# State update of the sample group: one matmul for each sample, on halves laid out by way of DRAM

## The chip, the cores and the metric

The kernel runs on one core of a Trainium2 chip. The metric is the device time of one execution in microseconds, the median of several runs. Engines are named as in the profile: PE is TensorE, DVE is VectorE, ACT is ScalarE, POOL is GpSimd, SP is SyncE, which here only issues DMAs.

## The reference

One layer of a hybrid decoder on 256 prompt tokens and 8 samples of 8 tokens each (64 sample tokens). An input projection of 2048 to about 13,000 columns feeds a Mamba-2 mixer (32 heads of 64, state 128, in 4 groups of 8 heads) and a gated short convolution; an output projection joins them. All is float32.

```python
h = rmsnorm(x, norm_w)
proj = jnp.einsum('bld,de->ble', h, w_in)
z_s, xbc, dt_raw, z_c, b_c, c_c, v_c = jnp.split(proj, SPLIT_POINTS, axis=-1)
xbc, buf_ssd_new = causal_dwconv(xbc, buf_ssd, conv_ssd_w)
xs, bm, cm = jnp.split(jax.nn.silu(xbc + conv_ssd_b), (D_SSM, D_SSM + SSD_GN), axis=-1)
y_s, h_new = ssd_scan(xs, dt, a, bm, cm, d_skip, h_ssm)
# inside ssd_scan:
states = jnp.einsum('bclgn,bclgh,bclghp->bcghpn', bc, decay_end, xdt)
h_next = h * chunk_decay + states
```

The last two lines are the state update that this case is about. For each sample b and each group g the new state is the old one times a decay, plus the sum over that sample's 8 tokens of the outer product of B (128 state columns) and the weighted x (512 columns, 8 heads of 64).

## The kernel before, in words

**Projections.** Tokens stand in the free dimension (256 + 64 = 320 columns). A product has one weight tile of 128 output columns and 16 steps of 128 along the contraction; each step is three matmuls (L175 to L177), since weights and activations are each split into a rounded part and a remainder (`wh`, `wl`; `xh`, `xl`) and three of the four cross products are taken. The weights come by SP's DMAs in halves of a tile (`wr`, three buffers, L150). ScalarE casts a quarter to `wh` (L159), VectorE subtracts to get `wl` (L160); six quarters of each can be held. So every quarter of every weight tile passes over SP, ScalarE and VectorE before TensorE can use it.

**Order of the work.** `schedule()` sets the order of the weight tiles: for each of the groups 0 to 3 the tiles B, C, x (four), z (four), and between them tiles of the short convolution (`sc`, `sv`, `sz`, `sb`). What a group's scan has to do stands in the generator `ssd_group`; `inproj` advances it by one `yield` at steps 5, 10 and 15 of each product (`tick`), so that the scan's small matmuls stand between those of the products. TensorE's order is that of the code. The other engines' order is set by the framework's scheduler, which moves instructions by its own costs; each engine and each DMA queue then works strictly in order.

**The scan of a group.** `padded` and `pad_samples` lay the 64 sample tokens out over 128 rows, each run of 16 tokens (two samples) twice: rows 0 to 15 of a quadrant of 32 and again rows 16 to 31. On these rows:
- `bt` is B transposed (tokens in rows). `Bst` holds, for each q in 0 and 1 (the even and the odd sample of a quadrant), B masked to that sample (`mq[q]`), as a rounded part and a negated remainder (ACT L595, DVE L596; 4 tiles of 128 x 128).
- `xw2` is the weighted x. `xst` has its rounded part in a quadrant's first 16 rows and the remainder in the last 16 (ACT L619 with the factor `sgn`, DVE L621 with `m1`).
- For each q, four matmuls `py` (L659) read the loaded old states `ht`, then for k = 0, 1 (rounded part and remainder of B) four matmuls `up` (L671), one in each quadrant of 32 rows, add up the update of four samples: two rounds of four. There is a block of this kind twice in a group, eight blocks in all.
- GpSimd multiplies `ht` by the decay (L675), VectorE adds `up` to `ht` (L682), GpSimd stores it (`out_hs`, L683).

**Around it.** SP also loads `ht` (`hload`, L554) and `R`, a row of cumulated decays broadcast to all rows (`rload`, L546). `rpart` turns R into decay factors: for the second chunk (c = 1) ScalarE takes an exponential into `CE` (L565) and GpSimd multiplies it by C (L566); then VectorE subtracts (L573, four heads to a tile), ScalarE takes the exponential (L576), VectorE multiplies by `CBm` (L577). `hf` is the prompt's final state, stored by `out_hp` (L653). In the same stretch stand the first short convolution's steps: `c` (L740), `pad` (L746, L748), `sa` (L753, L755), with GpSimd's copies L750 and L509.

Most of these 128 x 512 tiles come from one rotating pool of `NTR` = 12 tiles with the tag `tr` (`t5`, `small`).

Of the kernel before, what the change touches and what calls it, by code (L numbers as in the profile page):

```python
# [9 lines left out]
F32 = mybir.dt.float32  # L10
F32R = mybir.dt.float32r
AF = mybir.ActivationFunctionType
ALU = mybir.AluOpType
# [3 lines left out]
P = 128  # L17
# [3 lines left out]
NL = 8  # L21
TS = NB * NL
T = TP + TS
TQ = T // 4
KT = DM // P
H = 32
# [27 lines left out]

C_M1 = C_UP + TS
C_SG = C_M1 + 1
C_MQ = C_SG + 1
NC_ = C_MQ + 2

BEFORE = 2  # L60
BETWEEN = (1, 1, 1, 2)
# [3 lines left out]
NTR = 12  # L65
# [31 lines left out]
def hymba_step(ctx: ExitStack, tc: tile.TileContext, A, O):  # L97
    nc = tc.nc
    V, S, PE, GP, SP = nc.vector, nc.scalar, nc.tensor, nc.gpsimd, nc.sync

    def pool(name, bufs=1, **kw):
        return ctx.enter_context(tc.tile_pool(name=name, bufs=bufs, **kw))
# [6 lines left out]
    dr = pool("dram", space=DRAM)  # L109
# [4 lines left out]
    def bc(ap, shape):  # L114
        return ap.to_broadcast(shape)

    def win(t, at, *dims):

        v = t[:, at:at + 1]
        return bass.AP(v.tensor, v.offset, [v.ap[0], *[list(d) for d in dims]])  # L120
# [14 lines left out]
    def load(i):  # L135
        if i >= NTILE or i in raws:
            return
        got = []
        for hf in range(2):
            if i >= LATE and 2 * (i - LATE) + hf < 4 * NLATE - 3:  # L140
                r = keep[0].tile([P, KH, P], F32, name=f"wk{i}_{hf}")
            else:
                r = wp.tile([P, KH, P], F32, name=f"wr{i}_{hf}", tag="wr", bufs=3)
            if i < nin:
                src = A["w_in"][i, :, hf * KH:(hf + 1) * KH, :]
            else:
                d, part = divmod(i - nin, 2)
                k0 = part * KT + hf * KH
                src = A["w_out"][d, :, k0:k0 + KH, :]
            SP.dma_start(r, src)  # L150
            got.append(r)
        raws[i] = got
# [32 lines left out]
    xw = sp0.tile([P, KT, XW], F32, name="xw")  # L185
# [19 lines left out]
    load(NFIRST)  # L205
    con = cp.tile([P, NC_], F32, name="con")
    SP.dma_start(con, A["con"])
# [10 lines left out]
    UP = con[:, C_UP:C_UP + TS]  # L218
    m1 = con[:, C_M1:C_M1 + 1]
    sgn = con[:, C_SG:C_SG + 1]  # L220
    mq = [con[:, C_MQ + q:C_MQ + q + 1] for q in range(2)]
    cso = cp.tile([P, NXT, NB + 1, 3], F32, name="cso")
    sso = cp.tile([P, NSH, NB + 1, 2], F32, name="sso")
    ones = cp.tile([P, 1], F32, name="ones")
# [9 lines left out]
    for n in range(3):  # L234
        t = cp.tile([P, PW], F32, name=f"pad{n}")
# [35 lines left out]
    for k in range(KT):  # L271
        h = wp.tile([P, NFIRST * P], F32R, name=f"sh{k}", tag="wh", bufs=6)
# [112 lines left out]
    ssd = sst_.enter_context(tc.tile_pool(name="ssd", bufs=1, reuse_waits="tile"))  # L385
# [15 lines left out]
    acd = dr.tile([H, T], F32, name="acd")  # L401
    totd = dr.tile([H, NB + 1], F32, name="totd")

    seg = ssd.tile([H, T], F32, name="seg")
    GP.memset(seg, 1.0)
    GP.memset(win(seg, 0, (P, 2)), 0.0)
    GP.memset(win(seg, TP, (NL, NB)), 0.0)
    ges = ssd.tile([H, T], F32, name="ges")
    GP.memset(ges, 1.0)
    GP.memset(win(ges, P - 1, (P, 2)), 0.0)  # L410
    GP.memset(win(ges, TP + NL - 1, (NL, NB)), 0.0)
    CH = ((0, P, P), (P, P, P), (TP, TS, TS))

    def small(name, rows=H, cols=T):
        return ssd.tile([P, 512], F32, name=name, tag="tr", bufs=NTR)[:rows, :cols]

    def decays():

# [107 lines left out]
    def ssd_group(g, Bt, Ct, xs, zs):  # L526
# [3 lines left out]
        def t5(name, dt=F32):  # L530
            return ssd.tile([P, 512], dt, name=f"{name}_{g}", tag="tr", bufs=NTR)

        def tl(name):
            return ssd.tile([P, 512], F32, name=f"{name}_{g}", tag="tl", bufs=5)

        def rload(c, part):

            o, n, _ = CH[c]
            nh = 512 // n
            h0 = HPG * g + part * nh  # L540
            if (c, part) in PARTS[:2]:
                R = ssd.tile([P, 512], F32, name=f"R{c}_{part}_{g}", tag="rs", bufs=2)
            else:
                R = t5(f"R{c}_{part}")
            R = R.rearrange("p (h l) -> p h l", h=nh)
            SP.dma_start(R, bc(acd[h0:h0 + nh, o:o + n].rearrange("(u h) l -> u h l", u=1), [P, nh, n]))  # L546
            for h in range(nh):
                Rs[c, part * nh + h] = R, h

        hts = {}  # L550

        def hload(b):
            hts[b] = t5(f"ht{b}")
            SP.dma_start(hts[b], A["h"][g, :, b, :])  # L554
# [32 lines left out]
        p = sm(f"bt{g}")  # L587
# [2 lines left out]
        PE.transpose(p[:, 2 * P:3 * P], padded(Bt), ident)  # L590
        Btok = ssd.tile([P, 2 * P], F32, name=f"Btok{g}", tag="Btok")
        S.copy(Btok, p[:, :2 * P])
        Bst = ssd.tile([P, 2, 2, P], F32R, name=f"Bst{g}", tag="Bst")
        for q in range(2):
            S.activation(Bst[:, q, 0, :], p[:, 2 * P:3 * P], AF.Copy, scale=mq[q])  # L595
            V.scalar_tensor_tensor(out=Bst[:, q, 1, :], in0=p[:, 2 * P:3 * P], scalar=mq[q],  # L596
                                   in1=Bst[:, q, 0, :].bitcast(F32), op0=ALU.mult, op1=ALU.subtract)
        yield
        p = sm(f"cb{g}")
        CBm = ssd.tile([P, T], F32, name=f"CBm{g}", tag="CBm")  # L600
        for c, (o, n, _) in enumerate(CH):
            PE.matmul(p[:, o:o + n], Bt[:, o:o + n] if c < 2 else padded(Bt), Ct[:, o:o + n],
                      start=True, stop=True)
        V.tensor_tensor(out=CBm[:, :TP].rearrange("p (c l) -> p c l", c=2),
                        in0=p[:, :TP].rearrange("p (c l) -> p c l", c=2),
                        in1=bc(U.rearrange("p (o l) -> p o l", o=1), [P, 2, P]), op=ALU.mult)
# [4 lines left out]
        p = sm(f"xt2{g}")  # L611
# [3 lines left out]
        xw = t5("xw2")  # L615
        V.tensor_tensor(out=heads(xw, g), in0=heads(p, g), in1=perhead(w_tok[:, 2, hs]), op=ALU.mult)
        V.tensor_tensor(out=heads(xdt[2], g), in0=heads(p, g), in1=perhead(dt_tok[:, 2, hs]), op=ALU.mult)
        xh_ = t5("xh2", F32R)
        S.activation(xh_, xw, AF.Copy, scale=sgn)  # L619
        xst = ssd.tile([P, 512], F32R, name=f"xst{g}", tag="xst")  # L620
        V.scalar_tensor_tensor(out=xst, in0=xw, scalar=m1, in1=xh_.bitcast(F32), op0=ALU.mult, op1=ALU.add)  # L621
        yield
        rpart(0)
        yield
# [2 lines left out]
        for c in range(2):  # L627
            p = sm(f"xt{c}_{g}")
            for j in range(4):
# [3 lines left out]
                            in1=perhead(dt_tok[:, c, hs]), op=ALU.mult)  # L633
            xw = t5(f"xw{c}")
            V.tensor_tensor(out=heads(xw, g), in0=heads(p, g),
                            in1=perhead(w_tok[:, c, hs]), op=ALU.mult)
# [7 lines left out]
            p = sm(f"st{c}_{g}")  # L644
# [3 lines left out]
            else:  # L648
                hf = t5("hf")
                GP.tensor_tensor(out=heads(hf, g), in0=heads(h1, g),  # L650
                                 in1=decay(NB, g), op=ALU.mult)
# [5 lines left out]
        for q in range(2):  # L657
            for j in range(4):
                PE.matmul(py[32 * j:32 * j + 32, :], cz[:, 2 * j + q, :], hts[2 * j + q],  # L659
                          start=q == 0, stop=q == 1)  # L660
            if q == 0:
                for b in range(4):
                    hload(2 * b + 1)
            else:
                for part in PARTS[2:]:
                    rload(*part)
            ups = [sm(f"up{g}_{q}_{j}") for j in range(4)]
            for k in range(2):
                for j in range(4):
                    at = slice(32 * j, 32 * j + 32)  # L670
                    PE.matmul(ups[j], Bst[at, q, k, :], xst[at, :], start=k == 0, stop=k == 1)  # L671
            for j in range(4):
                b = 2 * j + q
                ht = hts[b]
                GP.tensor_tensor(out=heads(ht, g), in0=heads(ht, g),  # L675
                                 in1=decay(b, g), op=ALU.mult)
            yield
            yield
            for j in range(4):
                b = 2 * j + q  # L680
                ht = hts.pop(b)
                V.tensor_tensor(out=ht, in0=ht, in1=ups[j], op=ALU.add)  # L682
                GP.dma_start(O["hs"][g, :, b, :], ht)  # L683
                if j == 1:
                    yield
            yield
            yield
# [9 lines left out]
        for j in range(4):  # L697
            pd = sm(f"pd{g}_{j}")
            for c, (o, n, _) in enumerate(CH):
                for u in range(2):  # L700
                    h = 2 * j + u
                    PE.matmul(pd[u * HD:(u + 1) * HD, o:o + n], xdt[c][:, h * HD:(h + 1) * HD],  # L702
                              Rs[c, h][0][:, Rs[c, h][1], :], start=True, stop=c != 1)
                for u in range(2 * (c == 1)):
                    h = 2 * j + u
# [3 lines left out]
        for j, pd in enumerate(pds):  # L709
# [3 lines left out]
                                   in1=pd[:, :T], op0=ALU.mult, op1=ALU.add)  # L713
# [11 lines left out]
        v, a, b = (t5(f"{n}g")[:, :T] for n in "vab")  # L725
        yield from rms(acc, 4 * P, sm(f"rg{g}")[:, :T], [t5(f"acc{n}", F32R)[:, :T] for n in "hl"], v, a, b, b)
        yield
        for j in range(4):
            ct = 4 * g + j
            V.scalar_tensor_tensor(out=ysr[:, ct, :], in0=ys[j], scalar=vec[:, V_SN + ct:V_SN + ct + 1],  # L730
                                   in1=b, op0=ALU.mult, op1=ALU.mult)
# [53 lines left out]
    for i in [*range(2, NFIRST + NAHEAD), 0, 1, *range(NFIRST + NAHEAD, nin)]:  # L785
# [9 lines left out]
        if kind in "BC":  # L795
            t = ssd.tile([P, T + P], F32, name=f"{kind}{idx}", tag=kind, bufs=2)
# [4 lines left out]
        elif kind == "x":  # L801
            t = ssd.tile([P, T + P], F32, name=f"x{idx}", tag="xs", bufs=6)
# [58 lines left out]
    for d in range(KT):  # L861
        i = nin + 2 * d
        n = TP if i >= LATE else T
# [42 lines left out]
    t = tp.tile([P, T], F32, name="yt2", tag="yc")  # L906
    fnr, u, t = (a[late, :LW] for a in (fnr, u, t))
# [37 lines left out]
    for m, pt in enumerate(pts):  # L945
        at = slice(m * P, (m + 1) * P)
# [12 lines left out]
    for e, at in ((S, slice(0, half)), (SP, slice(half, 2 * half))):  # L959
        V.tensor_tensor(out=rs[:, at, :], in0=rs[:, at, :],  # L960
                        in1=bc(p3[:, :TS].rearrange("p (o t) -> p o t", o=1), [P, half, TS]), op=ALU.mult)
# [3 lines left out]
def constants():  # L965
    c = np.zeros((P, NC_), np.float32)
    i = np.arange(P)
    c[:, C_ID:C_ID + P] = np.eye(P)
    c[:, C_U:C_U + P] = i[:, None] <= i[None, :]
    t = np.arange(TS)  # L970

    tok, half = 16 * (i // 32) + i % 16, i // 16 % 2
    c[:, C_DI:C_DI + TS] = (half[:, None] == 0) & (tok[:, None] == t[None, :])
    c[:, C_UP:C_UP + TS] = (half[:, None] == 1) & (tok[:, None] // NL == t[None, :] // NL) & (tok[:, None] <= t[None, :])
    c[:, C_M1] = half
    c[:, C_SG] = 1 - 2 * half
    for q in range(2):
        c[:, C_MQ + q] = tok // NL % 2 == q
    return c


# [67 lines left out]
```

## Time and profile before

| | |
|---|---|
| median of 3 runs | 1027.83 us (1027.24 to 1028.45) |
| the profiled execution | 1028.2 us, its span 1026.4 us |
| TensorE clock granted | 0.998 |
| busy: PE, DVE, ACT, POOL | 1016.7, 671.5, 499.2, 199.8 us |
| DMA | 176.62 MB, 172 GB/s over the span |
| blocks of `py` and `up` | 8, from 143.5 to 491 us |

The profile is of one execution. Times of rows are microseconds from the start of the span; a duration of a single instruction is given in ns where it says so. In a timeline a row has start, length, engine, line, operation, the tile written and the tiles read, shapes, how many instructions were merged, and in brackets the engine's idle time before it and what ended it. A matmul's length is longer than the distance to the next one's start, since matmuls are pipelined. A wait is put down to what came last.

### The profile page before, as it was taken

To read this page: it belongs to the slowest core of one execution; us is meant where nothing else is said; L and a number is where in the kernel's file an instruction comes from. 1 tells how busy PE (TensorE), PEld (TensorE's weight loads), DVE (VectorE), ACT (ScalarE), POOL (GpSimd) and SP (SyncE) were. 2 spreads that over 40 slices of the span, in tenths; PEclk is the share of its full clock that TensorE was granted. 3 is DMA by queue.
4 is the path that set the end of the run, shared out by engine and by line. 5 is a ranking of instruction groups with operands and counts; after the bars stand their busy time and mean duration, and the time that the engine had idled before them with its cause. 6 is when DMAs were issued, how large, how long until landed. Compare 5 with 4: busy or idle time off the path is not lost.

```text
span 1026.4 us, 18690 instructions
## 1 busy us (share of the span) xinstructions
PE 1016.7 (99%) x7223; PEld 996.4 (97%) x7223; DVE 671.5 (65%) x1221; ACT 499.2 (49%) x901; POOL 199.8 (19%) x293
## 2 busy tenths in 40 slices
PE   9999999999999999999999999999999999999997
PEld 9999999999999989999999999999999999999996
DVE  7797767886978777886867555555556544444444
ACT  8476444663457444754445343443435544444450
POOL 0131034221522134224323100111111000000000
PEclk9999999999999999999999999999999999999999
DMA  9345474646473566458547444444445744544412
GB/s 370 126 135 180 145 264 167 185 143 227 167 224 124 195 217 212 137 167 257 186 150 244 158 146 154 153 144 154 155 145 156 259 150 145 154 154 145 149 37 103
DMA packets 63304, 176.62 MB, mean 172 GB/s; under 512 B 10496, under 2 KB 20352, under 8 KB 63088
## 3 DMA queue, kind: packets, MB, share of 16 engines
q1 hardware_dynamic: 59712, 164.98, 48.3%
q0 software_dynamic: 3072, 9.96, 2.7%
q8 instruction: 56, 0.92, 0.4%
q10 hardware_dynamic: 432, 0.49, 0.1%
q14 instruction: 32, 0.26, 0.1%
HBM read 162.83 MB, written 12.58 MB: 171 GB/s over the span
## 4 chain that ended last, share of the span: by engine, by line
PE 88%; DVE 5%; issue 3%; DMA 2%; POOL 1%; ACT 1%; DVEq 0%; SPq 0%; POOLq 0%; ACTq 0%
PE pj L176 20%; PE pj L175 20%; PE pj L177 20%; PE po L175 7%; PE po L177 7%; PE po L176 7%; PE pf L284 3%; DVE wl L160 1%; POOL ht L675 1%; DMA R<-acd 1%; PE pd L702 1%; DVE ht L682 1%; DVE R L573 1%; PE pt L918 1%; DVE R L577 1%
## 5 line engine op out<-in xcount | busy, mean ns | idle before, releaser
L160 DVE TENSOR_TENSOR wl<-wr,wh 128x512 fp32r<-128x512 f32 x518 | 364.8, 712 | 269.2 <-ACT wh L159 265.6
L159 ACT CAST wh<-wr 128x512 fp32r<-128x512 f32 x518 | 314.9, 618 | 387.5 <-PE pj L177 216.1
L175 PE MATMUL pj<-xh,wh 128*128 128x320 f32 x1600 | 499.6, 312 | 0.0
L176 PE MATMUL pj<-xh,wl 128*128 128x320 f32 x1600 | 493.8, 309 | 1.5 <-DVE wl L160 1.5
L177 PE MATMUL pj<-xl,wh 128*128 128x320 f32 x1600 | 493.2, 308 | 0.0
L175 PEld LDWEIGHTS pj<-xh,wh 128*128 128x128 f32 x1600 | 300.2, 188 | 5.6 <-issue 5.4
L176 PEld LDWEIGHTS pj<-xh,wl 128*128 128x128 f32 x1600 | 300.3, 188 | 4.6 <-DVE wl L160 2.7
L177 PEld LDWEIGHTS pj<-xl,wh 128*128 128x128 f32 x1600 | 300.2, 188 | 0.0
L176 PE MATMUL po<-ysh,wl 128*128 128x320 f32 (+1 forms) x256 | 78.3, 306 | 0.0
L177 PE MATMUL po<-ysl,wh 128*128 128x320 f32 (+1 forms) x256 | 78.3, 306 | 0.0
L175 PE MATMUL po<-ysh,wh 128*128 128x320 f32 (+1 forms) x256 | 78.3, 306 | 0.0
L175 PE MATMUL po<-ych,wh 128*128 128x320 f32 (+1 forms) x256 | 78.2, 306 | 0.0
L177 PE MATMUL po<-ycl,wh 128*128 128x320 f32 (+1 forms) x256 | 78.1, 305 | 0.0
L176 PE MATMUL po<-ych,wl 128*128 128x320 f32 (+1 forms) x256 | 78.1, 305 | 0.0
L175 PEld LDWEIGHTS po<-ysh,wh 128*128 128x128 f32 x256 | 48.2, 188 | 0.0
L175 PEld LDWEIGHTS po<-ych,wh 128*128 128x128 f32 x256 | 48.1, 188 | 0.0
L177 PEld LDWEIGHTS po<-ycl,wh 128*128 128x128 f32 x256 | 48.1, 188 | 0.0
L176 PEld LDWEIGHTS po<-ysh,wl 128*128 128x128 f32 x256 | 48.1, 188 | 0.0
L176 PEld LDWEIGHTS po<-ych,wl 128*128 128x128 f32 x256 | 48.1, 188 | 0.0
L177 PEld LDWEIGHTS po<-ysl,wh 128*128 128x128 f32 x256 | 48.1, 188 | 0.0
L894 POOL TENSOR_TENSOR acco<-acco,sqo 128x320 f32<-128x320 f32 x13 | 11.4, 881 | 186.7 <-ACT sqo L890 186.7
L518 DVE SCALAR_TENSOR_TENSOR cv<-pad,vec,cv 128x344 f32<-128x344 f32 x72 | 40.5, 569 | 4.0 <-ACT cv L516 3.1
(260 smaller groups left out, 919.8 us busy)
## 6 DMA issues: line engine op xcount, KB each, us to landing
wr<-in_w_in SPq DMA_DIRECT2D x200, 512.0 KB, 3.5
wr<-in_w_out SPq DMA_DIRECT2D x59, 512.0 KB, 3.7
ht<-in_h SPq DMA_DIRECT2D x32, 256.0 KB, 5.0
out_hs<-ht POOLq DMA_DIRECT2D x32, 256.0 KB, 2.9
R<-acd SPq DMA_DIRECT2D x20, 256.0 KB, 5.9
xw<-in_xw SPq DMA_DIRECT2D x6, 848.0 KB, 10.6
wk<-in_w_out SPq DMA_DIRECT2D x5, 512.0 KB, 6.2
resp<-in_xp SPq DMA_DIRECT2D x1, 2048.0 KB, 8.2
```

Source lines behind the costliest of these rows:

```text
L159: S.copy(h, r)
L160: V.tensor_sub(l, r, h.bitcast(F32))
L175: PE.matmul(ps, h, hi(k), start=start and k == 0, stop=False)
L176: PE.matmul(ps, l, hi(k), start=False, stop=False)
L177: PE.matmul(ps, h, lo(k), start=False, stop=stop and k == KT - 1)
L284: PE.matmul(ps0[i], w[:, i * P:(i + 1) * P], x[:, k, :], start=k == 0 and w is h and x is xh, stop=k == KT - 1 and w is l)
L518: V.scalar_tensor_tensor(out=a, in0=pad[:, k:k + CW], scalar=vec[:, w + k:w + k + 1], in1=a, op0=ALU.mult, op1=ALU.add)
L573: V.tensor_scalar(out=R[:, h, :], in0=R[:, h, :], scalar1=ac_tok[:, c, at:at + 1], scalar2=0.0, op0=ALU.subtract, op1=ALU.min)
L577: V.tensor_tensor(out=R, in0=R, in1=bc(CBm[:, o:o + n].rearrange("p (u l) -> p u l", u=1), [P, nh, n]), op=ALU.mult)
L675: GP.tensor_tensor(out=heads(ht, g), in0=heads(ht, g), in1=decay(b, g), op=ALU.mult)
L682: V.tensor_tensor(out=ht, in0=ht, in1=ups[j], op=ALU.add)
L894: GP.tensor_tensor(out=acc, in0=acc, in1=sq, op=ALU.add)
```

## The change: what it does

- A helper `halves` splits a tile by rows: the rounded part stays in the first 16 rows of a quadrant, the remainder in the last 16. It is used for x as before (now `xq`) and for B as well (`Bq`), in place of the four masked tiles; the masks `mq` go.
- `Bq` and `xq` are written to DRAM tiles `Bd` and `xd` by GpSimd, twice each, and read back by SP, for each q, into `Bst[q]` and `xst[q]`. There a quadrant's 32 rows belong to one sample: 8 tokens, four times over, with each of the four pairings of a half of B and a half of x.
- The loop over k goes: one `up` matmul for each sample, on 32 rows.
- `seg` and `ges`, two constant tiles of the decay stage, come from the rotating pool instead of having room of their own.

```diff
+        def halves(to, a):
+            h = t5(f"h{a.shape[1]}", F32R)[:, :a.shape[1]]
+            S.activation(h, a, AF.Copy, scale=sgn)
+            V.scalar_tensor_tensor(out=to, in0=a, scalar=m1, in1=h.bitcast(F32), op0=ALU.mult, op1=ALU.add)
...
+        Bd = dr.tile([4, 2, 2, 16, P], F32, name=f"Bd{g}")
+        xd = dr.tile([4, 2, 2, 16, 512], F32, name=f"xd{g}")
...
-        Bst = ssd.tile([P, 2, 2, P], F32R, name=f"Bst{g}", tag="Bst")
+        Bst = [None, None]
+        xst = [None, None]
+        Bq = t5("Bq", F32R)[:, :P]
+        halves(Bq, p[:, 2 * P:3 * P])
+        for n in range(2):
+            GP.dma_start(Bd[:, :, n], Bq.bitcast(F32))
         for q in range(2):
-            S.activation(Bst[:, q, 0, :], p[:, 2 * P:3 * P], AF.Copy, scale=mq[q])
-            V.scalar_tensor_tensor(out=Bst[:, q, 1, :], in0=p[:, 2 * P:3 * P], scalar=mq[q],
-                                   in1=Bst[:, q, 0, :].bitcast(F32), op0=ALU.mult, op1=ALU.subtract)
+            Bst[q] = ssd.tile([P, P], F32R, name=f"Bst{g}_{q}", tag="Bst", bufs=2)
+            SP.dma_start(Bst[q].bitcast(F32), Bd.rearrange("j h n (q t) m -> q j (h n) (t m)", q=2)[q])
...
-        xh_ = t5("xh2", F32R)
-        S.activation(xh_, xw, AF.Copy, scale=sgn)
-        xst = ssd.tile([P, 512], F32R, name=f"xst{g}", tag="xst")
-        V.scalar_tensor_tensor(out=xst, in0=xw, scalar=m1, in1=xh_.bitcast(F32), op0=ALU.mult, op1=ALU.add)
+        xq = t5("xq", F32R)
+        halves(xq, xw)
+        for n in range(2):
+            GP.dma_start(xd[:, n], xq.bitcast(F32))
+        for q in range(2):
+            xst[q] = ssd.tile([P, 512], F32R, name=f"xst{g}_{q}", tag="xst", bufs=2)
+            SP.dma_start(xst[q].bitcast(F32), xd.rearrange("j n h (q t) c -> q j (n h) (t c)", q=2)[q])
...
-            for k in range(2):
-                for j in range(4):
-                    at = slice(32 * j, 32 * j + 32)
-                    PE.matmul(ups[j], Bst[at, q, k, :], xst[at, :], start=k == 0, stop=k == 1)
+            for j in range(4):
+                at = slice(32 * j, 32 * j + 32)
+                PE.matmul(ups[j], Bst[q][at, :], xst[q][at, :], start=True, stop=True)
```

In three places the instructions of an engine stand otherwise than before. The rows are those of group 1 (the other groups read alike); a name like `R_1_1_3329` is the tile R of chunk 0, part 1, group 1, and `wl_0_3209` the first quarter of a weight tile.

SP's queue, from the second half of one weight tile to the loads of the odd samples' states. Before:

```order
L150 DMA wr_0_3006<-in_w_in 128x1024
L554 DMA ht_1_3042<-in_h 128x512
L554 DMA ht_1_3044<-in_h 128x512
L554 DMA ht_1_3046<-in_h 128x512
L554 DMA ht_1_3048<-in_h 128x512
L150 DMA wr_1_3008<-in_w_in 128x1024
L150 DMA wr_0_3098<-in_w_in 128x1024
```

Now:

```order
L608 DMA Bst_0_2859<-Bd_2840 128x1x128
L608 DMA Bst_1_2861<-Bd_2840 128x1x128
L149 DMA wr_1_2928<-in_w_in 128x1024
L149 DMA wr_0_3024<-in_w_in 128x1024
L636 DMA xst_0_2916<-xd_2841 128x1x512
L636 DMA xst_1_2918<-xd_2841 128x1x512
L560 DMA ht_1_3060<-in_h 128x512
L560 DMA ht_1_3062<-in_h 128x512
L149 DMA wr_1_3026<-in_w_in 128x1024
L560 DMA ht_1_3064<-in_h 128x512
L560 DMA ht_1_3066<-in_h 128x512
L149 DMA wr_0_3116<-in_w_in 128x1024
```

Four reads from DRAM stand ahead of the state loads, each pair behind the GpSimd writes that it waits for, and the next weight load has moved in between the state loads.

VectorE, from the first R tile of chunk 0 to the second weight quarter behind it. Before:

```order
L573 TENSOR_SCALAR R_1_1_3329<-R_1_1_3329,ac_tok 128x128 x4
L682 TENSOR_TENSOR ht_1_3042<-ht_1_3042,up_0_0_3168 128x512
L682 TENSOR_TENSOR ht_1_3044<-ht_1_3044,up_0_1_3169 128x512
L682 TENSOR_TENSOR ht_1_3046<-ht_1_3046,up_0_2_3170 128x512
L682 TENSOR_TENSOR ht_1_3048<-ht_1_3048,up_0_3_3171 128x512
L160 TENSOR_TENSOR wl_0_3209<-wr_0_3098,wh_0_3208 128x512
L577 TENSOR_TENSOR R_1_1_3329<-R_1_1_3329,CBm_2867 128x512
L740 TENSOR_TENSOR c_3202<-pj_3118,rb_467 128x320
L160 TENSOR_TENSOR wl_1_3213<-wr_0_3098,wh_1_3212 128x512
L573 TENSOR_SCALAR R_0_1_3331<-R_0_1_3331,ac_tok 128x128 x4
L573 TENSOR_SCALAR R_1_1_3333<-R_1_1_3333,ac_tok 128x128
L160 TENSOR_TENSOR wl_2_3217<-wr_1_3100,wh_2_3216 128x512
```

Now:

```order
L579 TENSOR_SCALAR R_1_1_3343<-R_1_1_3343,ac_tok 128x128 x3
L696 TENSOR_TENSOR ht_1_3060<-ht_1_3060,up_0_0_3186 128x512
L696 TENSOR_TENSOR ht_1_3062<-ht_1_3062,up_0_1_3187 128x512
L696 TENSOR_TENSOR ht_1_3064<-ht_1_3064,up_0_2_3188 128x512
L696 TENSOR_TENSOR ht_1_3066<-ht_1_3066,up_0_3_3189 128x512
L579 TENSOR_SCALAR R_1_1_3343<-R_1_1_3343,ac_tok 128x128
L159 TENSOR_TENSOR wl_0_3223<-wr_0_3116,wh_0_3222 128x512
L754 TENSOR_TENSOR c_3216<-pj_3136,rb_467 128x320
L159 TENSOR_TENSOR wl_1_3227<-wr_0_3116,wh_1_3226 128x512
L583 TENSOR_TENSOR R_1_1_3343<-R_1_1_3343,CBm_2879 128x512
L579 TENSOR_SCALAR R_0_1_3345<-R_0_1_3345,ac_tok 128x128 x2
L159 TENSOR_TENSOR wl_2_3231<-wr_1_3118,wh_2_3230 128x512
```

One of R's four subtractions has gone behind the four `ht` adds, and `c` and the weight quarter `wl_1` have come ahead of R's product with `CBm`.

TensorE, one block for q = 0. Before:

```order
L659 MATMUL py_3155<-ht_1_3048,cz 32x512
L671 MATMUL up_0_0_3168<-xst_2900,Bst_2846 128x512
L671 MATMUL up_0_1_3169<-xst_2900,Bst_2846 128x512
L671 MATMUL up_0_2_3170<-xst_2900,Bst_2846 128x512
L671 MATMUL up_0_3_3171<-xst_2900,Bst_2846 128x512
L671 MATMUL up_0_0_3168<-xst_2900,Bst_2846 128x512
L671 MATMUL up_0_1_3169<-xst_2900,Bst_2846 128x512
L671 MATMUL up_0_2_3170<-xst_2900,Bst_2846 128x512
L671 MATMUL up_0_3_3171<-xst_2900,Bst_2846 128x512
L175 MATMUL pj_3118<-xh,wh_2_3018 128x320
```

Now:

```order
L674 MATMUL py_3173<-ht_1_3066,cz 32x512
L685 MATMUL up_0_0_3186<-xst_0_2916,Bst_0_2859 128x512
L685 MATMUL up_0_1_3187<-xst_0_2916,Bst_0_2859 128x512
L685 MATMUL up_0_2_3188<-xst_0_2916,Bst_0_2859 128x512
L685 MATMUL up_0_3_3189<-xst_0_2916,Bst_0_2859 128x512
L174 MATMUL pj_3136<-xh,wh_2_3036 128x320
```

The second round of four is gone; everything else on TensorE stands as before.

More of the change, by code (lines that the diff above doesn't have):

```diff
@@ L56 @@
 C_SG = C_M1 + 1
-C_MQ = C_SG + 1
-NC_ = C_MQ + 2
+NC_ = C_SG + 1
 BEFORE = 2
@@ L220, in hymba_step @@
     sgn = con[:, C_SG:C_SG + 1]
-    mq = [con[:, C_MQ + q:C_MQ + q + 1] for q in range(2)]
     cso = cp.tile([P, NXT, NB + 1, 3], F32, name="cso")
@@ L402, in hymba_step, with small @@
     totd = dr.tile([H, NB + 1], F32, name="totd")
-    seg = ssd.tile([H, T], F32, name="seg")
+    def small(name, rows=H, cols=T):
+        return ssd.tile([P, 512], F32, name=name, tag="tr", bufs=NTR)[:rows, :cols]
+    seg = small("seg")
     GP.memset(seg, 1.0)
@@ L407, in hymba_step @@
     GP.memset(win(seg, TP, (NL, NB)), 0.0)
-    ges = ssd.tile([H, T], F32, name="ges")
+    ges = small("ges")
     GP.memset(ges, 1.0)
@@ L412, in hymba_step @@
     CH = ((0, P, P), (P, P, P), (TP, TS, TS))
-    def small(name, rows=H, cols=T):
-        return ssd.tile([P, 512], F32, name=name, tag="tr", bufs=NTR)[:rows, :cols]
     def decays():
@@ L976, in constants @@
     c[:, C_SG] = 1 - 2 * half
-    for q in range(2):
-        c[:, C_MQ + q] = tok // NL % 2 == q
     return c
```

## The prediction

> **What bounds the kernel now.** I read the busy times first, then who waited for whom on TensorE, then the timeline around those waits, and followed it back engine by engine. The numbered stretch is the second head group (g = 1, the numbers 0 to 3 below are groups); the other groups repeat it.
>
> ```profile
> PE 1016.7 (99%) x7223; PEld 996.4 (97%) x7223; DVE 671.5 (65%) x1221; ACT 499.2 (49%) x901; POOL 199.8 (19%) x293
> ```
> ```profile
> PE pj L176 <- DVE wl L160: 1.5, 4, 0.5
> ```
> ```profile
> 279.65 0.31 PE L175 MATMUL pj<-xh,wh 128*128 128x320 f32 x1
> ...
> 280.09 0.31 PE L175 MATMUL pj<-xh,wh 128*128 128x320 f32 x1
> 280.65 0.42 PE L176 MATMUL pj<-xh,wl 128*128 128x320 f32 x1 [0.25 <-DVE wl L160]
> ```
>
> TensorE is busy for 99% of the span, so an instruction less on it should be time less. But it waits four times, once in each group, for VectorE's low half of a weight quarter (`wl`). Matmuls start 0.147 us apart (three in 279.65 to 280.09), and here the next start comes after 0.56 us: 0.41 us lost, of which the profile calls 0.25 idle because the matmul before is still draining for 0.16. Over four waits that is 1.5 + 4 x 0.16 = 2.1 us. At these four places TensorE is not the bound; VectorE is. They come right behind the edited blocks, so what VectorE does there decides.
>
> ```profile
> 257.15 2.85 DVE L573 TENSOR_SCALAR R<-R,ac_tok 128x128 f32<-128x128 f32 x4 [2.06 <-DMA R<-acd]
> 259.93 2.47 DVE L682 TENSOR_TENSOR ht<-ht,up 128x512 f32<-128x512 f32 x4
> ...
> 262.92 3.44 DVE L577 TENSOR_TENSOR R<-R,CBm 128x512 f32<-128x512 f32 x1
> 266.28 0.48 DVE L740 TENSOR_TENSOR c<-pj,rb 128x320 f32<-128x320 f32 x1
> 267.28 1.06 DVE L573 TENSOR_SCALAR R<-R,ac_tok 128x128 f32<-128x128 f32 x5
> 270.94 0.69 DVE L577 TENSOR_TENSOR R<-R,CBm 128x512 f32<-128x512 f32 x1 [0.16 <-ACT R L576]
> 271.55 0.69 DVE L160 TENSOR_TENSOR wl<-wr,wh 128x512 fp32r<-128x512 f32 x1
> 272.15 0.42 DVE L746 TENSOR_TENSOR pad<-pj,c 128x256 f32<-128x256 f32 x1
> 273.35 1.17 DVE L755 SCALAR_TENSOR_TENSOR sa<-pad,vec,sa 128x336 f32<-128x336 f32 x2
> 279.30 0.69 DVE L682 TENSOR_TENSOR ht<-ht,up 128x512 f32<-128x512 f32 x1 [0.34 <-POOL ht L675]
> 279.91 1.29 DVE L160 TENSOR_TENSOR wl<-wr,wh 128x512 fp32r<-128x512 f32 x2
> ```
> ```profile
> 253.43 0.58 POOL L653 DMA_DIRECT2D out_hp<-hf  x1 [7.68 <-DVE hf L652]
> 255.61 4.12 POOL L675 TENSOR_TENSOR ht<-ht,dec 128x512 f32<-128x512 f32 x4 [1.59 <-PE py L659]
> 260.90 2.33 POOL L683 DMA_DIRECT2D out_hs<-ht  x4 [1.17 <-DVE ht L682]
> 263.24 2.56 POOL L566 TENSOR_TENSOR CE<-CE,C 128x512 f32<-128x512 f32 x2
> 274.68 0.52 POOL L509 COPY pad<-cst 128x24 f32<-128x24 f32 x1 [1.32 <-DVE sa L755]
> 275.15 4.12 POOL L675 TENSOR_TENSOR ht<-ht,dec 128x512 f32<-128x512 f32 x4
> ```
> ```profile
> 259.57 1.28 ACT L565 ACT_TABLE_LOAD   x1 [5.19 <-DMA out_hp<-hf]
> ```
>
> The three fences are VectorE's, GpSimd's and ScalarE's timeline (start, length, instruction, idle time before it and what ended it). Read from below: the late `wl` (279.91) stands on VectorE behind the last `ht` add (279.30), which waits for GpSimd's four decay products (275.15). Those stand in GpSimd's queue behind the copy L509, which waits for `sa` (273.35), which needs `pad` (272.15), which stands behind everything VectorE has done since R landed at 257.15. The largest piece there is one R product of 3.44 us; an undisturbed one takes 0.69. It lasts until both CE products of GpSimd (263.24 to 265.80) are over. This chain starts from R's landing, from the landing of out_hp that releases ScalarE's table load (259.57), and from the state matmuls of `py` (the decay products at 255.61). All of these lie before or beside the first edited matmuls, at 255.46.
>
> **The change, part by part.**
>
> *Matmuls.* Eight blocks lose one round of four each.
>
> ```profile
> 255.46 0.74 PE L671 MATMUL up<-xst,Bst 32*128 32x512 f32 x8
> 256.13 0.41 PE L175 MATMUL pj<-xh,wh 128*128 128x320 f32 x1
> ```
>
> Two rounds take 256.13 - 255.46 = 0.67, so a round is 0.33 and eight are 2.65 us, 0.66 in each group. From the streaming rate of the neighbours the low end is 0.147 x 512 / 320 = 0.235 a round, 1.9 us in all; I take 0.33, since it is the thing itself. The Trainium skill (TensorEngine Tiling, Key Properties) says that changing the tiling mode drains the engine; by that rule the drain is paid on entering and leaving a block, not per round, and only the streaming, 1.9 us, would leave. No run here shows which.
>
> Is it paid? In each group both edited blocks (255.46 and a second one some 14 us later) lie ahead of the wait at 280.65 and behind the start of the chain that ends it. If that chain keeps its length, TensorE arrives 0.66 earlier and waits 0.66 longer: gain nothing. So the gain of a group is what VectorE's chain gets shorter, up to 0.66 plus the wait that is there now.
>
> *VectorE's order.* The scheduler has moved its instructions in this very stretch. One subtraction of R goes behind the `ht` adds, and `c` and the next `wl` come ahead of the R product; the eight later subtractions stand closer together. Between the `ht` adds and `wl_0` of the next-but-one tile VectorE has the same work plus that subtraction. Three differences count:
> - The adds start when GpSimd's last decay product ends and the third subtraction is through, one subtraction (1.06 / 5 = 0.2) earlier. out_hs and the CE products follow on GpSimd, so the CE window ends 0.2 earlier.
> - `c` (0.4 from start to next start) reads PSUM and now runs before the window; the `wl` behind it is the one caught, instead of the R product. 0.4.
> - The 0.16 before the third R product goes: its exponential on ScalarE now follows subtractions that are all done one split earlier.
>
> Sum 0.76 for group 1, and I take it for 2 and 3 as well, since their order is the same and the longest R product (3441 ns in the second row below, min/median/max of all 20) is no longer than this one. Group 0 is different, in the first row:
>
> ```profile
> 152.00 2.11 DVE L160 TENSOR_TENSOR wl<-wr,wh 128x512 fp32r<-128x512 f32 x1 [0.61 <-ACT wh L159]
> ```
> ```profile
> L577 DVE TENSOR_TENSOR R<-R,CBm x20: 680/693/3441, 119.8 to 492.3; 128x512 f32<-128x512 f32 x20
> ```
>
> There VectorE waits for ScalarE's cast, so the 0.2 is lost and 0.56 is left. 3 x 0.76 + 0.56 = 2.84. Bounds: no gain if the caught instruction loses elsewhere what `c` wins; at most 2.65 + 2.1 = 4.8 us, when TensorE no longer waits at all. I take the 2.84, which lies nearest the rows.
>
> ScalarE has its two casts back to back ahead of R's exponential, which so starts one cast later; VectorE wants its result only after the caught `wl`, past 266, so this costs nothing.
>
> *Halves and DRAM.* One ScalarE and one VectorE instruction on B go away in each group, at 0.37 and 0.35 us:
>
> ```profile
> L595 ACT ACTIVATE Bst<-bt,con x8: 367/368/374, 116.8 to 450.1; 128x128 fp32r<-128x128 f32 x8
> L596 DVE SCALAR_TENSOR_TENSOR Bst<-bt,con,Bst x8: 342/350/351, 117.2 to 450.5; 128x128 fp32r<-128x128 f32 x8
> ```
> ```profile
> 234.90 0.74 DVE L621 SCALAR_TENSOR_TENSOR xst<-xw,con,xh 128x512 fp32r<-128x512 f32 x1
> ```
> ```profile
> 238.86 1.80 SPq L554 DMA_DIRECT2D ht<-in_h  x4
> 242.40 4.70 SPq L150 DMA_DIRECT2D wr<-in_w_in  x2
> 250.75 0.33 SPq L150 DMA_DIRECT2D wr<-in_w_in  x1
> 251.17 1.06 SPq L546 DMA_DIRECT2D R<-acd  x1
> ```
> ```profile
> out_hs<-ht POOLq DMA_DIRECT2D x32, 256.0 KB, 2.9
> ```
>
> (The fences below the first two rows are VectorE's and SP's timelines and a row of the DMA issues, with KB and us to landing.) The removed ones lie 20 us ahead of the chain: nothing. Four GpSimd DMAs to DRAM come in (0.58 each, by out_hs), in a stretch where GpSimd idles (7.68 before out_hp): nothing. SP gets four reads, and the x pair is the point: xq is ready when xst was, at 235.64; two issues of 0.58 and a landing of 2.9 give 239.7. SP, in order, holds there the `ht` loads (two of four issue some 1.5 us later, the other two behind the next weight load, past 242.8). It meets its next weight load at about 241.5, before that load's buffer is free at 242.40, so weights and R are not late. The reads land by 246 (`ht` takes 5.0) and are wanted at 255.46. Ahead of R's issue at 251.17 SP then has about 5.5 us of issues (1.8 for the x pair and two `ht` loads, 2.7 for the other six, 0.33 for each of three weight loads), so a landing up to 245.7, 6 us later than worked out, would still cost R nothing.
>
> The Trainium skill (SBUF — State Buffer, SBUF: two separate sides) warns that descriptors of a GpSimd DMA starve while VectorE holds the shared port, 3.1 us instead of 0.62. The out_hs row above, four in 2.33 beside VectorE's adds and `wl`, does not show it; by the rule, estimated, x would land near 245 and its reads would fall into the busy stretch below, which would turn the sum into that of the third rival.
>
> `seg` and `ges` move into the ring of 12 `tr` tiles, and each group draws three more tiles from it; the new waits that come of this are on the x write (239.7) and on stores of the group before, over when they are asked: nothing.
>
> Sum: the profiled execution's 1028.2 (its span 1026.4) less 2.84 is 1025.4; the median of the runs, 1027.83, is 0.4 under that execution, which gives **1025.0 us**.
>
> **Rivals.** What can be told from no change here is 0.2%, 2.1 us.
> 1. *The stall swallows all.* The chain keeps its length, and TensorE's 0.66 per group becomes waiting. For it: the chain's start, ahead of both edits. Against: `c` plainly moves. Gain 0 to 2, 1027.8 to 1025.8.
> 2. *TensorE-bound after all.* VectorE is no longer caught for the whole CE window (group 0's split, 2.11, came out sooner than the 3.44), and up to 2.76 (3.44 - 0.68) more comes off the chain. Then all of 2.65 + 2.1 counts: 1023.1.
> 3. *DMA pushed into the busy stretch: slower.*
>
> ```profile
> 246.00:247.00 1.00, 1.00 (x10) 0.99 (x9) 0.94 (x2) 0.03 (x1) 0.00 (x0) 1.00 0.09 33
> 247.00:248.00 1.00, 1.00 (x9) 1.00 (x8) 0.96 (x2) 0.40 (x1) 0.00 (x0) 1.00 0.27 45
> 248.00:259.00 11.00, 11.00 (x76) 9.12 (x75) 5.78 (x9) 2.46 (x5) 3.97 (x5) 1.00 0.93 314
> ```
>
> From 248 to 259 the DMA engines are 93% busy, and out_hp, which releases the table load, lands at that stretch's end. The x reads add 0.5 MB, 1.7 us at 314 GB/s. The idle 0.91 + 0.73 us ahead of it (246 to 248) takes about all of that. What it doesn't take moves R and out_hp later, one for one, in each group. Above 0.76 left over the kernel is slower; with all 1.7, 4 x (1.7 - 0.76) = 3.8 slower, 1031.6.
>
> **Chances and range.** Forecast (gain 2.1 to 3.6, so 1024.2 to 1025.7) 0.42; rival 1 0.31; rival 2 (above 3.6) 0.18; rival 3 0.09. Faster by over 0.2% are the forecast and rival 2: 0.60; within 0.2% rival 1: 0.31; slower 0.09. The range runs from rival 2's end to a little past rival 1's, 1023.0 to 1028.2.
>
> **What would show it.** Eight blocks of four matmuls with the next `pj` 0.33 after their start; four waits for `wl`, still there, in sum near 2.1 + 2.65 - 2.84 = 1.9 us; `pad` some 0.8 earlier after R's landing; a `wl` of 2 to 3 us where the R product of 3.44 was. Wrong would be: waits grown by 0.66 (rival 1), gone (rival 2), or R and out_hp landing more than 0.76 later against `py` (rival 3).

## The result: slower, 1050.88 us

| | us, median (lowest to highest) |
|---|---|
| before, beside the changed kernel | 1027.24 (1027.08 to 1028.45, 5 runs) |
| changed | 1050.88 (1048.63 to 1051.83, 5 runs) |
| ratio, estimated from the single runs (the two medians give 1.0230) | 1.0216, 95% interval 1.0205 to 1.0228 |

The profiled execution took 1051.83 us (span 1049.8), 23.4 us more span than before. The forecast was 1025.0, with a range up to 1028.2.

### The profile after

First the page's busy times and its chain of work, then the chain of the kernel before, then TensorE's waits (engine and line, what it waited for: us in sum, times, longest).

```profile
PE 1027.7 (98%) x7191; PEld 999.0 (95%) x7191; DVE 659.5 (63%) x1217; ACT 497.6 (47%) x897; POOL 209.9 (20%) x309
...
PE 83%; DMA 8%; DVE 4%; issue 2%; POOL 1%; ACT 1%; DVEq 0%; POOLq 0%; SPq 0%; ACTq 0%
```
```profile
PE 88%; DVE 5%; issue 3%; DMA 2%; POOL 1%; ACT 1%; DVEq 0%; SPq 0%; POOLq 0%; ACTq 0%
```
```profile
PE py L674 <- DMA ht<-in_h: 7.4, 4, 2.7
PE pj L175 <- DVE wl L159: 6.4, 8, 1.1
```

TensorE has 32 matmuls fewer and is busy 11 us longer, so its busy time is no measure of work here. DMAs make up 8% of the chain, against 2% before. The old wait for `wl` has grown from 1.5 us in four to 6.4 in eight, and there is a new one, for the loads of the old states (`ht`). TensorE's timeline at the first block of group 1:

```profile
259.84 1.55 PE L674 MATMUL py<-ht,cz 128*32 128x512 f32 x4
262.70 1.69 PE L674 MATMUL py<-ht,cz 128*32 128x512 f32 x4 [1.31 <-DMA ht<-in_h]
264.32 0.51 PE L685 MATMUL up<-xst,Bst 32*128 32x512 f32 x4
264.76 0.42 PE L174 MATMUL pj<-xh,wh 128*128 128x320 f32 x1
```
```profile
L674 PE MATMUL py<-ht,cz x64: 592/617/1062, 143.7 to 513.4; 128*32 128x512 f32 x64
```
```profile
L659 PE MATMUL py<-ht,cz x64: 592/605/617, 143.5 to 489.8; 128*32 128x512 f32 x64
```

(The last two rows are the view of that line's instructions, now and before, ns min/median/max.) The eight `py` products of this block take 4.5 us from 259.84 to 264.32, and single ones last up to 1062 ns. In the second block, where `ht` is there in time, they take 1.0 (278.79 to 279.78). In the whole run the weight loads ahead of `py` wait ten times for `ht`, 14.4 us in sum, partly at the same time as TensorE's own waits. Added up from start to next start over the four groups, `py` after `py` takes 19.9 us, against 3.8 before: 16.1 of the 23.4 us lost. From `pj` to the next `pj` it is 7.6 more in sum, from `py` to `up` 0.7 more, and the `up` blocks up to the next `pj` gave back 1.3.

Why is `ht` late? SP's timeline of the same group:

```profile
241.62 2.53 SPq L149 DMA_DIRECT2D wr<-in_w_in  x2
253.09 1.17 SPq L636 DMA_DIRECT2D xst<-xd  x2
254.31 1.05 SPq L560 DMA_DIRECT2D ht<-in_h  x2
255.46 0.38 SPq L149 DMA_DIRECT2D wr<-in_w_in  x1
255.93 0.86 SPq L560 DMA_DIRECT2D ht<-in_h  x2
...
262.67 2.60 SPq L550 DMA_DIRECT2D R<-acd  x3
```

After a weight load (its second one ends at 244.15) SP issues nothing for 8.9 us. It stands at the read of x, and behind it stand `ht` and R. What it waits for, in the view of SP's waits, and the rows of the DMA issues (KB each, median us to landing):

```profile
SPq L636 <- DMA xd<-xq: 35.0, 4, 9.1
```
```profile
ht<-in_h SPq DMA_DIRECT2D x32, 256.0 KB, 7.4
out_hs<-ht POOLq DMA_DIRECT2D x32, 256.0 KB, 3.0
R<-acd SPq DMA_DIRECT2D x20, 256.0 KB, 7.5
xd<-xq POOLq DMA_DIRECT2D x8, 256.0 KB, 9.6
```

GpSimd's write of x takes 9.6 us. out_hs, with the same 256 KB on the same queue, takes 3.0. There are two such writes in a group. In this one they go out at 241.25 and 241.95; the first lands at 250.08, the second at 253.03. The last two columns of the windows are the busy share of the 16 DMA engines and GB/s:

```profile
243.00:249.00 6.00, 6.00 (x42) 5.72 (x40) 3.98 (x7) 2.29 (x5) 0.00 (x0) 1.00 0.70 175
250.00:251.00 1.00, 1.00 (x9) 1.00 (x8) 0.00 (x0) 0.22 (x1) 0.93 (x1) 1.00 0.26 86
251.00:252.00 1.00, 1.00 (x9) 0.99 (x9) 0.57 (x1) 0.40 (x1) 0.13 (x1) 1.00 0.25 102
```

While weight loads and both writes are under way, the engines are 70% busy. When the second write and the rest of one weight load are left, they are a quarter busy, and SP still stands. A quarter of 16 engines is four. The write's pattern is 4x32x512, its outermost size 4; out_hs goes out as 128x512. By the Trainium skill (DMA: Bandwidth & Descriptors, Why a DMA increments its semaphore by 16 and not by 1), a DMA is spread over at most 16 engines, and their number has to divide the outermost size of both its sides: here 4. The trace agrees where one of the two writes is left: 0.25. How much of the 9.6 us comes of the few engines, and how much of the loads that share them, is not divided here.

### The profile page after: what moved, and what is told of

It is laid out like the page before. It is cut to its first block, busy times and chain, and to the rows that moved or that the text cites. A ratio compares the mean times of both kernels' runs of the same rounds, so it can differ in the third digit from the quotient of the medians.

```text
span 1049.8 us, 18679 instructions
## 1 busy us (share of the span) xinstructions
PE 1027.7 (98%) x7191; PEld 999.0 (95%) x7191; DVE 659.5 (63%) x1217; ACT 497.6 (47%) x897; POOL 209.9 (20%) x309
## 4 chain that ended last, share of the span: by engine, by line
PE 83%; DMA 8%; DVE 4%; issue 2%; POOL 1%; ACT 1%; DVEq 0%; POOLq 0%; SPq 0%; ACTq 0%
PE pj L175 19%; PE pj L174 19%; PE pj L176 18%; PE po L174 7%; PE po L176 7%; PE po L175 7%; DMA R<-acd 3%; PE pf L282 3%; DMA ht<-in_h 3%; DMA wr<-in_w_in 2%; DVE wl L159 1%; POOL ht L689 1%; PE pd L716 1%; DVE R L583 1%; DVE R L579 1%
## 5 line engine op out<-in xcount | busy, mean ns | idle before, releaser
L159 DVE TENSOR_TENSOR wl<-wr,wh 128x512 fp32r<-128x512 f32 x518 | 371.2, 724 | 289.6 <-ACT wh L158 285.8
L175 PEld LDWEIGHTS pj<-xh,wl 128*128 128x128 f32 x1600 | 300.9, 188 | 10.4 <-DVE wl L159 8.4
```

Of the source, the lines that this page charges most:

```text
L159: V.tensor_sub(l, r, h.bitcast(F32))
L175: PE.matmul(ps, l, hi(k), start=False, stop=False)
```

## The experiments

Theory A: the outermost size of 4 puts the x write on four engines; it lands late, SP stands in order behind it, and `ht`, R and the weights come late. B: descriptors of a GpSimd DMA starve behind VectorE's port, the rule that the prediction had weighed and set aside. C: the added bytes are the cost.

All medians, with the ratio to the kernel before run on the same chip:

| run | us | ratio (95%) |
|---|---|---|
| x write with outermost 8 | 1032.83 | 1.0045 (1.0030 to 1.0059) |
| one x write per quadrant | 1026.87 | 0.9989 (0.9980 to 0.9999) |
| x write issued by ScalarE | 1051.89 | 1.0243 (1.0225 to 1.0262) |
| reads of x later on SP | 1037.95 | 1.0102 (1.0083 to 1.0120) |
| one round, no transport | 1024.50 | 0.9962 (0.9950 to 0.9975) |
| before, plus the unread slow write | 1030.75 | 1.0024 (1.0014 to 1.0033) |
| per quadrant, reads placed later | 1027.10 | 0.9986 (0.9977 to 0.9995) |
| second round cut, order as before | 1027.68 | 0.9993 (0.9984 to 1.0002) |
| slow writes, reads of older data | 1029.03 | 1.0013 (1.0004 to 1.0022) |
| per quadrant, x read by GpSimd | 1025.93 | 0.9980 (0.9971 to 0.9989) |
| the same, B read by GpSimd too | 1026.22 | 0.9980 (0.9971 to 0.9989) |

### The shape of the write

**Outermost size 8.** The B write, with a quarter of the bytes, takes the 4 in exchange.

```diff
-            GP.dma_start(Bd[:, :, n], Bq.bitcast(F32))
+            GP.dma_start(Bd[:, n], Bq.bitcast(F32))
...
-            GP.dma_start(xd[:, n], xq.bitcast(F32))
+            GP.dma_start(xd[:, :, n], xq.bitcast(F32))
```

> The two halves change places: the write of x to DRAM has 8 as its outermost dimension instead of 4, that of B has 4 instead of 8; bytes, queues and the order of every engine stay. Theory A (a write whose outermost dimension is 4 keeps only 4 of the 16 DMA engines busy, lands 9.6 us after issue instead of 2.9, and holds SP's queue 8.9 us): x lands in about half the time, 5 to 6 us, SP's hold falls to 3 to 5 us, time 1030 to 1042. Theory B (GpSimd's DMAs are slow here because their descriptors starve while VectorE works): x lands as late as before, 1050. Theory C (the extra bytes fill the DMA engines): 1050.

**One write per quadrant**: eight DMAs of 32x512 in the place of two of 4x32x512.

```diff
-            GP.dma_start(xd[:, n], xq.bitcast(F32))
+            for j in range(4):
+                GP.dma_start(xd[j, n], xq[32 * j:32 * j + 32].bitcast(F32))
```

> x is written by eight DMAs of 32 rows in place of two of 4 x 32 rows (one for each quadrant and copy); the bytes are the same, the scheduler puts SP's reads of x behind the state loads. Theory A: with 32 as outermost dimension all 16 engines work, the last write lands about 8 x 0.65 + 2.5 = 8 us after the first issue but each within 3 us of its own, weights are not held up, and SP is held for less than 2 us: 1024 to 1029, with the four waits for wl that the prediction spoke of. Theory B: four times as many descriptor jobs on GpSimd, 1050 or more. Theory C: 1050.

The x write's row of the DMA issues, in the run with 8 and in the run per quadrant:

```profile
xd<-xq POOLq DMA_DIRECT2D x8, 256.0 KB, 5.8
```
```profile
xd<-xq POOLq DMA_DIRECT2D x32, 64.0 KB, 3.7
```

SP's wait for it with 8:

```profile
SPq L636 <- DMA xd<-xq: 14.6, 4, 4.1
```

The landing goes from 9.6 to 5.8 with twice the outermost size. With it SP's stand for x goes from 35.0 to 14.6 us, and 18 of the 23.6 us come back (1032.83); the order of every engine is that of the changed kernel, so the shapes alone do this. Per quadrant the loss is gone: 1026.87. The bytes are the same in all three, so C falls.

The run per quadrant differs in more than the shape: the scheduler also puts the reads of x behind four `ht` loads and a weight load on SP. And its median of 3.7 us is of single writes. The eight go out one after another, and in group 1 the last lands at 245.33, 10.4 us after the first was issued (234.93), not much sooner than the 11.8 of the changed kernel. So an earlier x is at most a part of why this run is fast; the section on hold or traffic comes back to it.

**The same write from ScalarE.**

```diff
-            GP.dma_start(xd[:, n], xq.bitcast(F32))
+            S.dma_start(xd[:, n], xq.bitcast(F32))
```

> The two writes of x keep their shape (4 x 32 rows) and are issued by ScalarE instead of GpSimd. Theory A: still 4 engines, so x lands 8 us or more after issue and the kernel stays slow, 1045 to 1060. Theory B: without GpSimd no descriptors starve, x lands in about 3 us, 1024 to 1030. Theory C: 1050.

```profile
SPq L636 <- DMA xd<-xq: 36.4, 4, 10.0
```

SP waits as long for the write from another engine's queue (36.4 against 35.0 us), and the time is the same, 1051.89. The change of queue moved a few instructions of SP and VectorE too, but the reads of x still stand ahead of `ht`. GpSimd's descriptors are not the cause: B falls.

### Hold or traffic

The write can cost in two ways: SP stands behind it, or it delays other packets on its four engines. Three runs divide these.

**Reads later.** The code of the x reads moves to just ahead of `py`; on SP they then come behind four `ht` loads and a weight load, in the very order of the run per quadrant, with the slow write.

> The writes stay as they are; SP's two reads of x stand later in the code, just ahead of the py block, and the scheduler puts them behind the first four state loads and one more weight load. Theory A in its narrow form (all of the loss is SP standing still ahead of the state and R loads): x still lands 9 us after issue, SP is held for 2 us or less, 1025 to 1032. If the loss is rather that four engines are busy with x and the weights' packets on them are late: SP's hold is gone but the weights still land late, 1036 or more.

**The slow write alone**, in the kernel before; nobody reads it.

```diff
+        xd = dr.tile([4, 2, 2, 16, 512], F32, name=f"xd{g}")
+        for n in range(2):
+            GP.dma_start(xd[:, n], xst.bitcast(F32))
```

> The kernel before with one thing added: GpSimd writes xst to DRAM in two DMAs of 4x32x512 per group, and nothing reads it or waits for it. If the hold on SP was the whole loss, this costs nothing: same as before, within 2 us. If the slow write by itself delays the packets of weights, ht and R that share its four engines, it costs about what the run with the late reads lost, 10 us: 1036 to 1040, with a wr load of 10 us beside the write and waits for wl of 6 or more in sum.

**All transfers, but no wait.**

```diff
-            SP.dma_start(xst[q].bitcast(F32), xd.rearrange(...
+            SP.dma_start(xst[q].bitcast(F32), xold.rearrange(...
```

> The changed kernel with all its transfers, the slow 4x32x512 writes too, but each group's reads of x take the copy that the group before wrote (the first group one written at the start), so that no read waits for the write beside it. The sums of the states are then those of other data. VectorE's order is that of the changed kernel; the scheduler issues the reads earlier. If SP's hold behind the late landing is what costs (hold theory), this is near the kernel without transport (1024.5) plus the price of the write alone (2.5): 1026 to 1031. If the slow write costs mainly by sharing four engines with the other loads, the loss stays: 1040 or more.

The write's landing in the second of these; then SP's timeline in the second (two rows) and the third (three):

```profile
xd<-xst POOLq DMA_DIRECT2D x8, 256.0 KB, 9.7
```
```profile
239.42 5.29 SPq L554 DMA_DIRECT2D ht<-in_h  x4
...
252.09 2.72 SPq L546 DMA_DIRECT2D R<-acd  x3
```
```profile
237.68 5.62 SPq L569 DMA_DIRECT2D ht<-in_h  x4
...
246.05 3.00 SPq L569 DMA_DIRECT2D ht<-in_h  x4
...
250.33 2.66 SPq L557 DMA_DIRECT2D R<-acd  x3
```

The unread write costs 2.5 us (1030.75 against 1028.26), neither the nothing nor the 8 to 12 that were expected. With all transfers and no read waiting, 1029.03: the slow writes are there, `ht` goes out at 237.68 and R at 250.33, not at 254.31 and 262.67, and 21.9 of the changed kernel's 1050.88 are gone. The reads have also moved behind the `ht` loads on SP, so neither their wait nor their place holds SP any more: the hold is the cause of most of the loss, and the traffic the smaller part. Against the run without transport below (1024.50), 4.5 us are left. One place where the traffic costs is seen: issuing four `ht` loads takes SP 5.29 and 5.62 us beside the slow write, against 1.80 before. The run with later reads lies between, at 1037.95, in the range that was expected of traffic. But the premise of that range, SP's hold gone, did not come about; its waits of SP, and its first `ht` loads and R in group 1:

```profile
SPq L670 <- DMA xd<-xq: 10.1, 4, 3.0
```
```profile
239.94 5.81 SPq L560 DMA_DIRECT2D ht<-in_h  x4
...
257.11 2.45 SPq L550 DMA_DIRECT2D R<-acd  x3
```

The four loads take 5.81 us to issue, and then SP stands for x too. It stands less, since it comes to the reads later, but R goes out late; what each of the two costs here was not divided. The run per quadrant has the same order on SP; its waits and its timeline there:

```profile
SPq L637 <- DMA xd<-xq: 13.3, 6, 3.4
```
```profile
237.88 2.19 SPq L560 DMA_DIRECT2D ht<-in_h  x4
...
245.54 1.17 SPq L637 DMA_DIRECT2D xst<-xd  x2
...
250.18 2.72 SPq L550 DMA_DIRECT2D R<-acd  x3
```

It stands even longer, 13.3 us, where less than 2 had been expected. But its first four `ht` loads take 2.19 us to issue, the reads go out at 245.54 in this group, and R at 250.18, earlier than in the kernel before. The order of the engines is the same in these two runs, only the shape and number of the writes differ, and the times lie 11 us apart. It is not the length of a stand that costs, but whether it ends before what is behind it is due.

### What is left without the transport

**One round, no transport**: before, with `for k in range(1)`. The scheduler gives VectorE the changed kernel's order, word for word but for the halves.

> The kernel before with only the first of the two rounds (k = 0) in each block: the product with B's low half is left out, and nothing goes over DRAM. VectorE's order becomes that of the changed kernel. If the prediction's terms for VectorE hold and only the transport was wrong, this gives the forecast, a gain of 2.8 us on some 1028, about 1025.2; from the run with one write per quadrant, 2.5. If the stall swallows what TensorE saves (rival 1), 1026 to 1028. If TensorE bounds (rival 2), the blocks' 1.9 and the waits' 2.1 both go: 1024. Sum of the four waits for wl by the first: near 1.5; the blocks 0.43 us to the next pj.

**The second round cut to 128 of 512 columns**: VectorE's order stays that of before.

```diff
-                    PE.matmul(ups[j], Bst[at, q, k, :], xst[at, :], start=k == 0, stop=k == 1)
+                    w = slice(0, 512 if k == 0 else 128)
+                    PE.matmul(ups[j][:, w], Bst[at, q, k, :], xst[at, w], start=k == 0, stop=k == 1)
```

> The kernel before with the second round of each block cut to the first 128 of its 512 columns: the low half's product is left out for the other 384. VectorE's order stays word for word that of the kernel before; only TensorE gets shorter, by about 0.18 us a block (three quarters of 0.24), 1.4 us in eight. If the stall swallows what TensorE saves while VectorE's chain is unchanged, the same as before within 0.5 us and the four waits grow by 0.35 each; if the chain starts from the blocks too, up to 1.4 us faster.

All of TensorE's listed waits in the first (the three are from the start and the end of the program), and the one for `wl` in the second:

```profile
PE rft L955 <- DVE rgr L307: 2.9, 1, 2.9
PE pjw L243 <- DVE warm L190: 1.1, 1, 1.1
PE pf L284 <- ACT sh L260: 0.3, 1, 0.3
```
```profile
PE pj L176 <- DVE wl L160: 2.0, 3, 0.7
```

With VectorE's new order the waits for `wl` are gone and 3.8 us are won. Added up from start to next start, the blocks are 1.8 us shorter there and the stops between `pj` matmuls 2.1, together the whole gain. With the old order a shorter TensorE waits longer (1.5 to 2.0 in sum, though in three groups instead of four), and the time can't be told from before. From start to next start its blocks are 1.4 us shorter and the stops 0.7 longer: in the profiled execution the stall swallows half, as rival 1 would have it of all. So VectorE's order is what takes the waits away, and without it only a part of what TensorE saves can be seen. The new order with both rounds kept was not run.

### A better version

**Per quadrant, reads placed later.** The scheduler made of this the same order on VectorE, ScalarE, GpSimd and SP as of the run per quadrant.

> The run with one write per quadrant (1026.9), with the reads of x placed behind four ht loads and one weight load on SP. SP then no longer stands for x (13.3 us in that run). If what is left of the hold costs time, this is faster, 1025 to 1026; if it is covered, the same 1026.9 within 1 us. If late reads cost by themselves (they land some 8 us later, beside R), slower, 1028 or more, with waits for wl above the 1.6 of that run.

It is thus a second measurement of that version: 1027.10 beside 1026.87; it says nothing on the reads' place.

**x read by GpSimd**, behind its own writes, and then **B too**.

```diff
-            SP.dma_start(xst[q].bitcast(F32), xd.rearrange(...
+            GP.dma_start(xst[q].bitcast(F32), xd.rearrange(...
```

> The run with one write per quadrant (1026.9), with the two reads of x issued by GpSimd behind its own writes instead of by SP. SP then doesn't stand for x (13 us there) and has 8 issues less; GpSimd stands some 3 us in a stretch where it was idle until out_hp. If the rest of the hold and of the issues on SP makes the 2.4 us that this version is behind the kernel without transport (1024.5), 1024.5 to 1025.5; if it is the traffic of writes and reads itself, the same 1026.9 within 0.7; if reads issued by GpSimd land late (beside the adds of VectorE), up waits for xst and it is slower, 1030 or more.

> As the run before it, with the reads of B issued by GpSimd too, so that SP waits for no transport at all (another 11 us of standing on SP gone). If those stands on SP cost anything, up to 1 us faster than the run with x alone, 1024 to 1025; if they were covered, the same. GpSimd stands 3 to 4 us for B's landing ahead of the x writes; if x then comes later than up wants it (255), slower by that.

GpSimd's timeline in the first of them, group 1:

```profile
235.09 3.98 POOL L634 DMA_DIRECT2D xd<-xq  x8 [4.17 <-DVE xq L538]
245.64 1.07 POOL L637 DMA_DIRECT2D xst<-xd  x2 [6.57 <-DMA xd<-xq]
246.70 1.09 POOL L666 TENSOR_TENSOR hf<-h,dec 128x512 f32<-128x512 f32 x1
252.65 0.59 POOL L669 DMA_DIRECT2D out_hp<-hf  x1 [4.86 <-DVE hf L668]
```

GpSimd now stands for x, 6.57 us where some 3 had been expected, and still idles 4.86 before out_hp. This version, at 1025.93, beats the kernel before by 0.20% (0.11 to 0.29) and the changed one by 25 us, with the whole computation in it. It is 1.2 us ahead of the same version with the reads on SP (1027.10 on the same chip), though the intervals of the two ratios overlap. Reading B there too changes nothing (1026.22). What keeps it 1.4 us behind the run without transport wasn't tried.

## Why the prediction was wrong

**The failed step** is in the part on halves and DRAM: "two issues of 0.58 and a landing of 2.9 give 239.7". The 2.9 is the row of out_hs, chosen by queue and bytes; the shape, which sets how many DMA engines work, was not compared. It measured 9.6. In group 1 the writes go out at 241.25, 5.6 us later than worked out since group 0 has lost time already, and the reads at 253.09, when the second write has landed: 11.8 us, where the term had 4.1. SP stood there for x 8.9 us in this group and 35.0 in all, and in the run where no read waits 21.9 us of the time were gone.

**The slack was too large.** The prediction held that a landing 6 us late "would still cost R nothing", and this one is 7.7 late. But it counted 5.5 us of issues from the landing to R; that stretch took 9.6 (253.09 to 262.67), with issues of 7.8 and waits between them. And it named the `ht` loads as held and gave them no slack of their own; `py` wants them, and there most of the time was lost.

**Rival 3** had the right sign and a wrong mechanism: it was not the bytes of the reads that moved R but SP's stand, at the end of which the DMA engines were a quarter busy. With all the bytes and no stand for x the time is 1029.03. Its 1031.6 was priced by bytes. The starving descriptors were rightly set aside, on the wrong row: nothing in the out_hs row could show what a 4x32x512 write does. So "slower" had 0.09 for a case that no rival held.

**Matmuls.** 0.33 us a round was too much. `pj` follows a block of four after 0.44 (264.32 to 264.76), and it followed two rounds after 0.67: a round is 0.23, eight are 1.8 us. That is close to the low end, the streaming; the other 0.2 stays with each block. (Two blocks of the changed kernel took 0.73, so that it got 1.3 and not 1.8; in the run without transport all eight take 0.44.) The rule of the Trainium skill (TensorEngine Tiling, Key Properties) that the drain comes with a change of the tiling mode fits these numbers.

**VectorE's order** was right in kind and too small. Its timeline in the run without transport:

```profile
256.49 2.30 DVE L573 TENSOR_SCALAR R<-R,ac_tok 128x128 f32<-128x128 f32 x3 [2.60 <-DMA R<-acd]
258.71 2.47 DVE L682 TENSOR_TENSOR ht<-ht,up 128x512 f32<-128x512 f32 x4
...
262.30 2.84 DVE L160 TENSOR_TENSOR wl<-wr,wh 128x512 fp32r<-128x512 f32 x1
265.07 0.68 DVE L577 TENSOR_TENSOR R<-R,CBm 128x512 f32<-128x512 f32 x1
...
270.24 0.42 DVE L746 TENSOR_TENSOR pad<-pj,c 128x256 f32<-128x256 f32 x1
```

A `wl` of 2.84 stands where the R product of 3.44 was, as forecast. `pad` comes 13.75 us after the first subtraction, against 15.00 before: 1.25 earlier, not 0.76. The adds start 2.22 after that row, against 2.78: the subtraction that moved away took 0.56 here, beside GpSimd's decay products, and I had priced it at 0.2 from a calm stretch. With 1.25 the waits vanish, which is the state of rival 2: the blocks' 1.8 and the waits' 2.1 give 3.9, and 3.8 were measured. The forecast's 2.84 was too small: in the run without the transport it is rival 2, a gain above 3.6, that came true.

## What to carry to other kernels

Price a DMA by a row of the same shape: its outermost size first, bytes and queue second, and split a write whose outermost size is small into several that start from the rows; here the issue of the loads beside it also slowed less (2.19 us for four against 5.81). A read that waits for a write belongs on a queue with nothing urgent behind it; ask of everything behind it, one by one, who wants it and when. Fewer matmuls ahead of a wait can bring less than they save; look at what decides the wait.

## What was unexpected of the hardware

- 256 KB to DRAM landed in 9.6 us with an outermost size of 4 and in 5.8 with 8; out_hs, with 128, took 3.0. The weight load that SP issues in the changed kernel at 243.81, beside that write, took 10.4 us to land (the row below, of that line's DMAs between 243 and 245), against a median of 3.5 of all.

```profile
DMA to landing us min/median/max: 10.4/10.4/10.4
```

- Beside such a write the issue of a DMA on SP itself is slower: 1.3 to 1.4 us for each `ht` load (5.29 / 4 and 5.62 / 4), against 0.45.
- The page's busy time of TensorE rose by 11 us with 32 matmuls fewer: products whose operands came one by one stretched, up to 1062 ns (before: at most 617).
